# Four of the eight block sums per set of a 7-product SwiGLU layer moved from VectorE to accumulating SBUF transfers, the products reordered, and two more weight buffers

## The chip, the cores and the metric

The kernel runs on one core of a Trainium2 chip. The metric is the device time of one execution in microseconds (us). TensorE (PE) multiplies, with its weight loads as a sequence of their own (PEld); VectorE (DVE) and ScalarE (ACT) work element by element; GpSimd (POOL) and SyncE (SP) issue transfers (DMA). Each engine takes its instructions in order, and semaphores hold it back until what it needs is there.

## The reference, cut to what matters

A trunk of 4 layers over 256 tokens of width 1024. Each layer has an FFN, a token mixer with memory attention, and a second FFN, each wrapped in RMS norms:

```python
def swiglu_ffn(x, w_gate_up, w_down):
    gate, up = jnp.split(x @ w_gate_up, 2, axis=-1)
    return (jax.nn.silu(gate) * up) @ w_down
...
for i in range(DEPTH):
    x = x + 0.5 * rms_norm(swiglu_ffn(rms_norm(x, g[0]), ffn_w_gate_up[i, 0], ffn_w_down[i, 0]), g[1])
    h = rms_norm(x, g[2])
    ...
    x = x + rms_norm(y, g[3])
    x = x + 0.5 * rms_norm(swiglu_ffn(rms_norm(x, g[4]), ffn_w_gate_up[i, 1], ffn_w_down[i, 1]), g[5])
```

The hidden width of the FFN is 2816, everything is fp32, and there are 8 FFNs. The change is in the FFNs alone, but for the place in which some small tiles of other parts lie.

## The kernel before, in words

**Units of weight.** The weights are read once, in units of 512 KB (128 partitions x 1024 fp32). SP's queue loads a unit (L240) into one of `RAW` = 3 buffers named `raw`. ACT rounds it to a high part `hi` (L309) and DVE takes the rest as a low part `lo` (L310), both in rings of `RING` = 10 buffers. A product is then three matmuls, hi*hi, lo*hi and hi*lo (L334 to L336). `pump` (called from `slot`, after every unit that PE has taken) issues splits as far ahead as the ring has free places. A split of a `raw` frees that buffer and issues the next load of a `raw`.

**An FFN.** The 2816 hidden columns are done in 6 sets, 0 to 5, of 512 columns (the last of 256). For an ordinary set PE makes the gate half `g` (4 units) and the up half `u` (4 units) in PSUM banks named `rot`, of which there are 4; ACT and DVE make silu(gate) * up from them in tiles `T` (L537, L538, L727). PE transposes T (`turned`, L557) two units later, and the hidden columns go through the down matrix into two double banks `acc` (L684, `fill(n)`: n units of the down matrix, 24 matmuls for two). These fills are put between other products, so that PE has work while something is waited for.

**The seven-product sets.** Sets 2 and 4 of each FFN (`SEVEN`), 16 sets in all, do gate and up together as a 2x2 block product with 7 instead of 8 block products (`seven`, L626 to L661). The four weight blocks b11, b12, b21, b22 lie in four tiles `quad` of two halves of 512 KB each, 8 loads per set, which `slot` issues in the order b11, b21, b12, b22 (`load_quad`). The left operands are input blocks or sums of these (`sums`, made once per FFN, L599). The right operands are blocks or sums of them, made in place by `operand` with a DVE addition of 128x1024 (L277) for each half: b11+=b12, b11+=b22, b12+=b22, b21+=b11, so 8 additions per set. Each product, numbered op 0 to 6, is split like any unit and takes 12 matmuls of 512 columns, 6 for each half (L615). PE's order in a set is: op 0 into bank a; op 1 into bank b; the transposes of the set before (two banks); op 2 into bank c; op 3 into bank a; fill(2); op 4 into a; fill(2); op 5 into a; op 6 into c. DVE and ACT take from them: a snapshot P1 of a (ACT, L623), P1+b (DVE, L635, which reads bank b for the last time), a snapshot U2, a snapshot U3, c-U3 (DVE, L646), the silu of a and a product (L653), c-U2 (L658) and the product that gives the first half of T (L659).

Each engine's instructions are put in order by a scheduler when the program is built; within that, the order comes from the Python code and from the plan of units (`ffn_chunks`), by which the splits are issued. A bank, ring place or buffer is reused as soon as its last reader is done.

**Around it.** A boundary between stages makes norms and transposes (L373 to L385, L399). `gain` loads the norm gains. `setup2` loads and prepares the memory for the mixers. `mem_chunk` loads pieces of the memory into `memraw`.

Of the kernel before, what the change touches and what calls it, by code (L numbers as in the profile page):

```python
# [10 lines left out]
F32 = mybir.dt.float32  # L11
# [22 lines left out]
RAW = 3  # L34
# [27 lines left out]
def ffn_chunks(l, f):  # L62
# [8 lines left out]
    for s in range(SETS):  # L71
        if s in SEVEN:
            for ops, n in (((0, 1, 2, 3), 2), ((4,), 2), ((5, 6), 0)):
                order += [("S", l, f, s, op, h) for op in ops for h in range(2)]
                fill(n)
            continue
# [127 lines left out]
class Trunk:  # L204
# [53 lines left out]
    def load_quad(self):  # L258
# [16 lines left out]
    def operand(self, op, h):  # L275
        b11, b12, b21, b22 = (t if t is None else t[:, h, :] for t in self.quad)
        add = lambda x, y: self.nc.vector.tensor_tensor(out=x, in0=x, in1=y, op=ALU.add)  # L277
# [73 lines left out]
    def gain(self, l, n, tag):  # L351
        t = self.main.tile([P, D], F32, tag=tag, name=tag)
# [3 lines left out]
    def ln_stages(self, st, t, ps, post_scale, post_eps, gpost, gpre):  # L356
# [3 lines left out]
        junk = lambda: self.main.tile([P, D], BF16, tag="junk", name="junk")  # L360
# [11 lines left out]
        def s1():  # L372
            nc.scalar.activation(out=junk(), in_=ps, func=AF.Square, scale=post_scale, accum_out=ss)  # L373
# [6 lines left out]
        def s3():  # L380
            nc.scalar.activation(out=junk(), in_=x, func=AF.Square, scale=1 / 32, accum_out=ss2)
# [47 lines left out]
    def setup(self):  # L429
# [4 lines left out]
        self.gpre = self.gain(0, 0, "gpre")  # L434
# [18 lines left out]
    def setup2(self):  # L453
# [3 lines left out]

        def loads():
# [3 lines left out]
        def squares(t):  # L462
            m = self.main.tile([P, D], F32, tag="gpost", name="memrow")
            nc.sync.dma_start(out=m, in_=io["mem"][t * P:(t + 1) * P, :])
            ss = self.small.tile([P, 1], F32, tag="ss", name="ss", bufs=8)
            nc.scalar.activation(out=self.main.tile([P, D], BF16, tag="junk", name="junk"), in_=m, func=AF.Square,
# [3 lines left out]
        def inverse():  # L470
            ps = self.rot()
            for t in range(2):
                d = self.main.tile([P, SEQ], F32, tag="memraw", name="memf", bufs=2)
# [55 lines left out]
    def ffn(self, l, f, post_next, pre_next, last=False):  # L529
        nc, tc = self.nc, self.tc  # L530
        with tc.tile_pool(name=f"ffn{l}{f}", bufs=1, reuse_waits="tile") as fp:
# [61 lines left out]
            def sums():  # L593
# [3 lines left out]
                for dst, a, b, op in ((x22, x21, x22, ALU.subtract), (x21, x11, x21, ALU.subtract),  # L597
                                      (x11, x22, x11, ALU.subtract), (x12, x12, x11, ALU.add)):
                    tt(out=dst, in0=a, in1=b, op=op)  # L599
                    y = tuple(fp.tile([P, 4, P], F32R, tag=n, name=n, bufs=4) for n in ("sh", "sl"))  # L600
# [6 lines left out]
                return a11, a12, S1, S2, S3, a22, S4  # L607
# [721 lines left out]
```

## Time and profile before

| what | us |
|---|---|
| median of 3 runs | 1900.68 (1900.43 to 1908.29) |
| profiled execution | 1902.04 |
| its span, first to last instruction | 1900.2 |
| PE busy | 1858.8 (98%) |
| DVE busy | 1514.9 (80%) |
| ACT busy | 1085.9 (57%) |
| POOL busy | 59.8 (3%) |
| mean granted TensorE clock | 0.999 |

The span of the profiled execution is 1.84 us shorter than its time, which has what lies around the span too. A row of instruction groups in the profile gives line, engine, operation, out <- in, shape and count, then busy time, mean of one in ns, and the idle time of that engine just before them with what ended it. The lines of SP issue transfers ("SPq"); "us to landing" is from the issue to the data being there. In a timeline the columns are start, duration and the instruction; several like ones in a row are one line (x8), and idle time just before is in brackets. Consecutive matmuls overlap, so their start times and not their durations show the pace.

### The profile page before, as it was taken

The numbers are of one execution on the slowest core, as the hardware profiler recorded it, in microseconds if no ns is written. First come the engines' busy times: TensorE is split into PE (matmuls) and PEld (weight loads), VectorE is DVE, ScalarE is ACT, GpSimd is POOL, SyncE is SP. The second block draws the span as 40 slices with busy tenths as digits, with TensorE's granted clock in tenths as the row PEclk, the third lists the DMA queues.
The fourth block names the chain that finished last, engine by engine and source line by source line (L and its number), as shares of the span: only waits on it lengthen the run. The fifth ranks groups of instructions, "written<-read, shape, count | busy, mean of one in ns | idle before, by whom it ended". The sixth has DMA issues, their size and how long they took to land.

```text
span 1900.2 us, 25015 instructions
## 1 busy us (share of the span) xinstructions
PE 1858.8 (98%) x9406; PEld 1550.4 (82%) x9406; DVE 1514.9 (80%) x1828; ACT 1085.9 (57%) x1469; POOL 59.8 (3%) x115
## 2 busy tenths in 40 slices
PE   7999999999999999999999999999999999999998
PEld 5888888787878897888888889888888878988886
DVE  6987888896879768889697966878877886878894
ACT  5655656564656545655565656555556555656562
POOL 0000100000000000000000000000000000100000
PEclk9999999999999999999999999999999999999999
DMA  8646747545663663754566357275476535747632
GB/s 295 235 167 200 233 156 266 205 140 176 233 222 115 199 203 111 266 198 145 180 231 233 112 185 238 102 246 184 151 229 227 189 127 183 243 156 244 220 105 86
DMA packets 103865, 362.65 MB, mean 191 GB/s; under 512 B 12084, under 2 KB 16576, under 8 KB 103616
## 3 DMA queue, kind: packets, MB, share of 16 engines
q1 hardware_dynamic: 103568, 359.47, 56.5%
q8 instruction: 74, 1.21, 0.3%
q0 software_dynamic: 176, 1.59, 0.2%
q14 instruction: 47, 0.39, 0.1%
HBM read 359.95 MB, written 1.06 MB: 190 GB/s over the span
## 4 chain that ended last, share of the span: by engine, by line
PE 60%; DVE 17%; DMA 12%; ACT 5%; issue 4%; POOL 1%; ACTq 0%; SPq 0%; DVEq 0%
PE acc L684 15%; DMA raw<-in_w 12%; PE rot L615 9%; PE rot L334 9%; PE rot L336 9%; PE rot L335 9%; DVE lo L310 9%; ACT hi L309 4%; DVE quad L277 3%; PE acc L944 3%; PE rot L557 1%; PE rot L399 1%; PE rot L848 1%; DVE x L378 1%; PE rot L880 1%
## 5 line engine op out<-in xcount | busy, mean ns | idle before, releaser
L310 DVE TENSOR_TENSOR lo<-raw,hi 128x1024 fp32r<-128x1024 f32 (+1 forms) x515 | 624.4, 1219 | 216.9 <-ACT hi L309 207.5
L309 ACT ACTIVATE hi<-raw 128x1024 fp32r<-128x1024 f32 (+1 forms) x515 | 542.1, 1055 | 397.0 <-DMA raw<-in_w 259.0
L334 PE MATMUL rot<-hi,xth 128*128 128x512 f32 (+3 forms) x1072 | 414.9, 387 | 2.5 <-ACT hi L309 1.6
L336 PE MATMUL rot<-hi,xtl 128*128 128x512 f32 (+3 forms) x1072 | 411.6, 384 | 1.2 <-DVE xtl L310 1.1
L335 PE MATMUL rot<-lo,xth 128*128 128x512 f32 (+3 forms) x1072 | 411.6, 384 | 0.0
L309 ACT ACTIVATE hi<-quad 128x1024 fp32r<-128x1024 f32 x224 | 232.7, 1056 | 156.5 <-DVE quad L277 83.4
L310 DVE TENSOR_TENSOR lo<-quad,hi 128x1024 fp32r<-128x1024 f32 x224 | 269.4, 1220 | 7.2 <-ACT hi L309 6.2
L334 PEld LDWEIGHTS rot<-hi,xth 128*128 128x128 f32 x1072 | 202.1, 189 | 41.4 <-ACT hi L309 2.1
L336 PEld LDWEIGHTS rot<-hi,xtl 128*128 128x128 f32 x1072 | 201.9, 188 | 41.3 <-DVE xtl L310 2.3
L335 PEld LDWEIGHTS rot<-lo,xth 128*128 128x128 f32 x1072 | 202.1, 189 | 38.2
L684 PE MATMUL acc<-lo,hh 128*128 128x512 f32 x640 | 198.9, 390 | 0.0
L684 PE MATMUL acc<-hi,hh 128*128 128x512 f32 x640 | 198.0, 390 | 0.0
L684 PE MATMUL acc<-hi,hl 128*128 128x512 f32 x640 | 197.2, 389 | 0.0
L277 DVE TENSOR_TENSOR quad<-quad 128x1024 f32<-128x1024 f32 x128 | 154.2, 1220 | 0.9
L684 PEld LDWEIGHTS acc<-hi,hl 128*128 128x128 f32 x640 | 120.1, 188 | 25.0 <-DVE hl L310 0.2
L684 PEld LDWEIGHTS acc<-lo,hh 128*128 128x128 f32 x640 | 120.2, 188 | 24.8
L684 PEld LDWEIGHTS acc<-hi,hh 128*128 128x128 f32 x640 | 119.5, 188 | 24.3
L615 PE MATMUL rot<-hi,sh 128*128 128x512 f32 x256 | 103.0, 402 | 6.8 <-DVE snap L635 6.8
L615 PE MATMUL rot<-lo,sh 128*128 128x512 f32 x256 | 100.0, 391 | 0.0
L615 PE MATMUL rot<-hi,sl 128*128 128x512 f32 x256 | 97.4, 390 | 0.0
L374 DVE TENSOR_TENSOR rows<-acc,gpost 128x1024 f32<-128x1024 f32 x24 | 29.3, 1222 | 74.9 <-ACT junk L373 74.8
L615 PE MATMUL rot<-hi,xtl 128*128 128x512 f32 x192 | 74.8, 389 | 0.0
(212 smaller groups left out, 2439.8 us busy)
## 6 DMA issues: line engine op xcount, KB each, us to landing
raw<-in_w SPq DMA_DIRECT2D x504, 512.0 KB, 4.3
quad<-in_w SPq DMA_DIRECT2D x128, 512.0 KB, 5.8
gpre<-in_norm_g SPq DMA_DIRECT2D x12, 512.0 KB, 5.1
gpost<-in_norm_g SPq DMA_DIRECT2D x12, 512.0 KB, 5.4
memraw<-in_mem_t SPq DMA_DIRECT2D x32, 128.0 KB, 3.2
raw<-in_w SPq DMA_DIRECT2D x8, 384.0 KB, 3.5
sw<-in_sw SPq DMA_DIRECT2D x2, 768.0 KB, 8.1
cb<-cd POOLq DMA_DIRECT2D x1, 1536.0 KB, 9.9
```

Of the source, the lines that this page charges most:

```text
L277: add = lambda x, y: self.nc.vector.tensor_tensor(out=x, in0=x, in1=y, op=ALU.add)
L309: self.nc.scalar.activation(out=hi, in_=src, func=AF.Copy)
L310: self.nc.vector.tensor_tensor(out=lo, in0=src, in1=hi.bitcast(F32), op=ALU.subtract)
L334: mm(out, a[0], b[0], start=start, stop=False)
L335: mm(out, a[0], b[1], start=False, stop=False)
L336: mm(out, a[1], b[0], start=False, stop=stop)
L374: nc.vector.tensor_tensor(out=rows(), in0=ps, in1=gpost, op=ALU.mult)
L378: nc.vector.scalar_tensor_tensor(out=x, in0=rows(), scalar=r, in1=x, op0=ALU.mult, op1=ALU.add)
L399: nc.tensor.transpose(ps[:, (k - k0) * P:(k - k0 + 1) * P], rows[:, k * P:(k + 1) * P], self.ident)
L615: nc.tensor.matmul(ps, a[i], w[j][:, kk, :], start=fresh and h == kk == i == j == 0, stop=h == kk == i == 1, skip_group_check=True)
L684: mm(ys[t][:, n * 512:(n + 1) * 512], x, y[:, 0, n * 512:(n + 1) * 512], start=(j == 0 and x is a[0] and y is w[0]), stop=(j == NF - 1 and ...
L944: self.nc.tensor.matmul(o["y"][t][:, h * 512:(h + 1) * 512], x, y[:, 0, h * 512:(h + 1) * 512], start=(j == 0 and x is a[0] and y is w[0]) ...
```

## The change

**What it does.** Of the four sums of weight blocks per set, two are made by transfers: `gather` issues from GpSimd's queue a transfer from one SBUF tile into another with accumulation. b12+=b22 is issued for each half right after the load of b22's half; b21+=b11 after DVE's addition for op 2. That is 4 transfers of 512 KB per set, 64 in all. DVE keeps b11+=b12 (op 2; b12 has b22 in it by then) and gets b11-=b22 (op 4, a subtraction), together 4 instructions per set, so 64 in place of 128. Since op 2 needs b22 now, splits from op 2 on are held until all 8 loads of the set have been issued (`quads_for`).

The order of products changes: op 2, 3 and 4 are now S2 times (b11+b12+b22), S3 times (b12+b22) and S1 times (b11+b12). Op 2 goes into bank a, followed by fill(2); op 3 goes into bank a; a new bank c is taken only then, for op 4; op 5 goes into a, op 6 into c; and fill(2) closes the set.

Tiles are put elsewhere: `junk` and `memraw` share the four `snap` buffers, the gains lie in the buffers of the left sums (tag `S`, which replaces `sh` and `sl`) or in tiles of the mixer, and `memrow` lies in `rows`. The loads of the gains and `setup2` are issued after the second seven-product set of an FFN. `RAW` is 5 instead of 3.

```diff
-RAW = 3
+RAW = 5
...
-            for ops, n in (((0, 1, 2, 3), 2), ((4,), 2), ((5, 6), 0)):
+            for ops, n in (((0, 1, 2), 2), ((3, 4, 5, 6), 2)):
...
         self.fetch(self.quad[q][:, h, :], key)
+        if q == 3:
+            self.gather(self.quad[1][:, h, :], self.quad[3][:, h, :])
+
+    def gather(self, x, y):
+        self.nc.gpsimd.dma_start(out=x, in_=y, accum_op=ALU.add)
...
-        return max(0, len(self.quad_loads) - (QUADS - (2 * min(key[4], 3) + key[5] + 1)))
+        return max(0, len(self.quad_loads) - (QUADS - ((2 * key[4] if key[4] < 2 else 6) + key[5] + 1)))
...
-        add = lambda x, y: self.nc.vector.tensor_tensor(out=x, in0=x, in1=y, op=ALU.add)
         if op == 2:
-            add(b11, b12)
-        elif op == 3:
-            add(b11, b22)
+            self.nc.vector.tensor_tensor(out=b11, in0=b11, in1=b12, op=ALU.add)
+            self.gather(b21, b11)
         elif op == 4:
-            add(b12, b22)
-        elif op == 5:
-            add(b21, b11)
-        return (b11, b21, b11, b11, b12, b21, b22)[op]
+            self.nc.vector.tensor_tensor(out=b11, in0=b11, in1=b22, op=ALU.subtract)
+        return (b11, b21, b11, b12, b11, b21, b22)[op]
...
-    def gain(self, l, n, tag):
-        t = self.main.tile([P, D], F32, tag=tag, name=tag)
+    def dump(self):
+        return self.main.tile([P, D], BF16, tag="snap", name="junk", bufs=4)
+
+    def gain(self, l, n, t):
...
-                return a11, a12, S1, S2, S3, a22, S4
+                return a11, a12, S2, S3, S1, a22, S4
...
-                a, b, c = self.rot(), self.rot(), self.rot()
+                a, b = self.rot(), self.rot()
...
                 turned(s - 1)
-                product(s, 2, c, True)
-                product(s, 3, a, False, keep("U2"))
+                product(s, 2, a, False, keep("U2"))
                 fill(2)
+                product(s, 3, a, False, keep("U3"))
+                c = self.rot()
 
                 def c22():
-                    v["U3"] = snap(a)
                     tt(out=v["U3"], in0=c, in1=v["U3"], op=ALU.subtract)
 
-                product(s, 4, a, False, c22)
-                fill(2)
+                product(s, 4, c, True, c22)
...
                 product(s, 6, c, False, c12)
+                fill(2)
...
-            if (l, f) != (0, 0):
-                self.bg.append(gains)
...
+                    if s == max(SEVEN):
+                        self.bg.append(gains)
+                    if s == max(SEVEN) and (l, f) == (0, 0):
+                        self.bg.extend(self.setup2())
```

**How it moves the instructions.** The places are in set 2 of the second FFN of layer 2, here called set 10, since ten seven-product sets come before it. A number after a name is that of the buffer's tile, and what stands in brackets is what the instruction waits for: a semaphore of an engine (Activation is ACT), of a loading queue (DMAHW) or of a GpSimd transfer (DMASW).

On PE before, from the transposes of the set before on; rot_11760 is bank a, rot_11761 is b, rot_11762 is c, and the two between are those of the transposes:

```order
L557 MATMUL rot_11816<-ident_74,T_11510 128x128 [waits DVE_49]
L557 MATMUL rot_11816<-ident_74,T_11510 128x128 x3
L557 MATMUL rot_11823<-ident_74,T_11511 128x128 [waits DVE_49]
L557 MATMUL rot_11823<-ident_74,T_11511 128x128 x3
L615 MATMUL rot_11760<-hi_11716,sh_11499 128x512 [waits Activation_49]
L615 MATMUL rot_11760<-lo_11717,sh_11499 128x512
L615 MATMUL rot_11760<-hi_11716,sl_11500 128x512
L615 MATMUL rot_11760<-hi_11716,sh_11499 128x512
L615 MATMUL rot_11760<-lo_11717,sh_11499 128x512
L615 MATMUL rot_11762<-hi_11682,sh_11489 128x512 [waits DVE_49]
L615 MATMUL rot_11762<-lo_11683,sh_11489 128x512
L615 MATMUL rot_11762<-hi_11682,sl_11490 128x512
```

The first matmul of op 2, into bank c, waits for DVE, which has to free a bank; the scheduler has put 5 of op 3's matmuls into bank a ahead of it. On PE in the changed kernel at the same place, where rot_11739 is bank a:

```order
L563 MATMUL rot_11790<-ident_74,T_11489 128x128 [waits DVE_49]
L563 MATMUL rot_11790<-ident_74,T_11489 128x128 x3
L563 MATMUL rot_11797<-ident_74,T_11490 128x128 [waits DVE_49]
L563 MATMUL rot_11797<-ident_74,T_11490 128x128 x3
L622 MATMUL rot_11739<-hi_11659,sums_11480 128x512 [waits Activation_49]
L622 MATMUL rot_11739<-lo_11660,sums_11480 128x512
L622 MATMUL rot_11739<-hi_11659,sums_11480 128x512 x2
L622 MATMUL rot_11739<-lo_11660,sums_11480 128x512
```

Op 2 follows the transposes in bank a, and waits for ACT alone (its `hi`, and the snapshot P1). On PE in the changed kernel, the end of op 5 and the first matmul of op 6, where rot_11886 is bank c, which op 4 has filled:

```order
L622 MATMUL rot_11739<-hi_11810,xtl_11162 128x512
L622 MATMUL rot_11739<-hi_11810,xth_11161 128x512
L622 MATMUL rot_11739<-lo_11811,xth_11161 128x512
L622 MATMUL rot_11739<-hi_11810,xtl_11162 128x512
L622 MATMUL rot_11886<-hi_11822,sums_11484 128x512 [waits DVE_49]
```

Op 6 adds to bank c and waits for DVE, which reads that bank in L653 (c-U3, L646 before). The 12 matmuls of op 5 lie between op 4 and op 6; before, they were op 5's and those of a fill.

On DVE before, from the second split of op 0 to the last sums of the second half; quad_11526 is b11, quad_11585 b21, quad_11626 b12, quad_11663 b22:

```order
L310 TENSOR_TENSOR lo_11629<-quad_11526,hi_11628 128x1024 [waits PE_49,Activation_49]
L277 TENSOR_TENSOR quad_11526<-quad_11526,quad_11626 128x1024 [waits DMAHW6_49,DVE_49]
L310 TENSOR_TENSOR lo_11646<-quad_11585,hi_11645 128x1024 [waits Activation_49]
L277 TENSOR_TENSOR quad_11526<-quad_11526,quad_11626 128x1024 [waits DMAHW2_49,DVE_49]
L310 TENSOR_TENSOR lo_11666<-quad_11585,hi_11665 128x1024 [waits Activation_49]
L277 TENSOR_TENSOR quad_11626<-quad_11626,quad_11663 128x1024 [waits DVE_49]
L310 TENSOR_TENSOR lo_11683<-quad_11526,hi_11682 128x1024 [waits Activation_49]
L277 TENSOR_TENSOR quad_11626<-quad_11626,quad_11663 128x1024 [waits DVE_49]
L277 TENSOR_TENSOR quad_11526<-quad_11526,quad_11663 128x1024 [waits DVE_49]
L310 TENSOR_TENSOR lo_11700<-quad_11526,hi_11699 128x1024 [waits Activation_49]
L277 TENSOR_TENSOR quad_11585<-quad_11585,quad_11526 128x1024 [waits DVE_49]
L310 TENSOR_TENSOR lo_11717<-quad_11526,hi_11716 128x1024 [waits Activation_49]
```

All eight sums of a set stand here and in the rows behind, each with a wait for a load or for DVE's own result. On DVE in the changed kernel, where quad_11505 is b11, quad_11560 b21, quad_11601 b12, quad_11638 b22:

```order
L283 TENSOR_TENSOR quad_11505<-quad_11505,quad_11601 128x1024 [waits DMASW2_49,DVE_49]
L544 SCALAR_TENSOR_TENSOR T_11490<-T_11490,rot_11492 128x512 [waits Activation_49]
L311 TENSOR_TENSOR lo_11604<-quad_11505,hi_11603 128x1024 [waits DMAHW7_49,PE_49,Activation_49]
L311 TENSOR_TENSOR lo_11621<-quad_11560,hi_11620 128x1024 [waits Activation_49]
L283 TENSOR_TENSOR quad_11505<-quad_11505,quad_11601 128x1024 [waits DMASW3_49,DVE_49]
L311 TENSOR_TENSOR lo_11642<-quad_11560,hi_11641 128x1024 [waits Activation_49]
L311 TENSOR_TENSOR lo_11660<-quad_11505,hi_11659 128x1024 [waits Activation_49]
L286 TENSOR_TENSOR quad_11505<-quad_11505,quad_11638 128x1024 [waits DMAHW1_49,DMASW4_49,DVE_49]
L311 TENSOR_TENSOR lo_11678<-quad_11505,hi_11677 128x1024 [waits Activation_49]
L286 TENSOR_TENSOR quad_11505<-quad_11505,quad_11638 128x1024 [waits DMAHW4_49,DMASW5_49,DVE_49]
L311 TENSOR_TENSOR lo_11696<-raw_11456,hi_11695 128x1024 [waits DMAHW7_49,Activation_49]
L735 TENSOR_TENSOR T_11489<-T_11489,rot_11624 128x512 [waits PE_49]
```

Additions (L283) and subtractions (L286) now wait for GpSimd's transfers: the additions for b12+=b22, the subtractions for b21+=b11, which reads b11 before the subtraction may write it. Behind the last of them stand a split and the L735 that makes the T which PE's transposes (L563) read.

On SP the last load of the set, b22's second half, stands in this place right behind the load of the `raw` whose buffer comes free with the last split of a `raw` that DVE makes ahead of the set's first block (lo_11563, two rows of `hl` ahead of the first split of b11). It stands so in sets 0, 1, 2, 10 and 14; in the others it stands about ten loads earlier.

More of the change, by code (lines that the diff above doesn't have):

```diff
@@ L359, in ln_stages @@
             st["rows"] = None
-        junk = lambda: self.main.tile([P, D], BF16, tag="junk", name="junk")
         ss = self.small.tile([P, 1], F32, tag="ss", name="ss", bufs=8)
@@ L372, in s1 @@
         def s1():
-            nc.scalar.activation(out=junk(), in_=ps, func=AF.Square, scale=post_scale, accum_out=ss)
+            nc.scalar.activation(out=self.dump(), in_=ps, func=AF.Square, scale=post_scale, accum_out=ss)
             nc.vector.tensor_tensor(out=rows(), in0=ps, in1=gpost, op=ALU.mult)
@@ L380, in s3 @@
         def s3():
-            nc.scalar.activation(out=junk(), in_=x, func=AF.Square, scale=1 / 32, accum_out=ss2)
+            nc.scalar.activation(out=self.dump(), in_=x, func=AF.Square, scale=1 / 32, accum_out=ss2)
             self.rsqrt(r2, ss2, self.eps1)
@@ L433, in setup @@
         nc.sync.dma_start(out=self.x[0], in_=io["x"][:P, :])
-        self.gpre = self.gain(0, 0, "gpre")
+        self.gpre = self.gain(0, 0, self.main.tile([P, 2, D], F32, tag="mgh", name="gpre")[:, 0, :])
         nc.sync.dma_start(out=self.ident, in_=io["ident"])
@@ L456, in setup2 @@
         self.R = c.tile([P, SEQ], F32, name="R")
+        both = []
         def loads():
@@ L462, in squares @@
         def squares(t):
-            m = self.main.tile([P, D], F32, tag="gpost", name="memrow")
+            if t == 0:
+                both.append(self.main.tile([P, 2, D], F32, tag="rows", name="memrow"))
+            m = both[0][:, t, :]
             nc.sync.dma_start(out=m, in_=io["mem"][t * P:(t + 1) * P, :])
             ss = self.small.tile([P, 1], F32, tag="ss", name="ss", bufs=8)
-            nc.scalar.activation(out=self.main.tile([P, D], BF16, tag="junk", name="junk"), in_=m, func=AF.Square,
+            nc.scalar.activation(out=self.dump(), in_=m, func=AF.Square,
                                  scale=1 / 32, accum_out=ss)
@@ L472, in inverse @@
             for t in range(2):
-                d = self.main.tile([P, SEQ], F32, tag="memraw", name="memf", bufs=2)
+                d = self.main.tile([P, SEQ], F32, tag="snap", name="memf", bufs=4)
                 nc.vector.tensor_scalar(out=d[:, :P], in0=self.ident, scalar1=self.r_mem[:, t:t + 1], scalar2=None,
@@ L599, in sums @@
                     tt(out=dst, in0=a, in1=b, op=op)
-                    y = tuple(fp.tile([P, 4, P], F32R, tag=n, name=n, bufs=4) for n in ("sh", "sl"))
+                    y = fp.tile([P, 2, 4, P], F32R, tag="S", name="sums", bufs=4)
+                    y = (y[:, 0], y[:, 1])
                     self.split(*(v.rearrange("p a b -> p (a b)") for v in y), dst)
@@ L667, in gains @@
             def gains():
-                gn["post"] = self.gain(l, post_next[0], "gpost")
+                tile = lambda n: fp.tile([P, D], F32, tag="S", name=n, bufs=4)
+                gn["post"] = self.gain(l, post_next[0], tile("gpost"))
                 if pre_next:
-                    gn["pre"] = self.gain(*pre_next, "gpre")
-            if (l, f) != (0, 0):
-                self.bg.append(gains)
+                    gn["pre"] = self.gain(*pre_next, tile("gpre"))
             ys = [self.acc() for _ in range(2)]
@@ L706, in ffn @@
                     seven(s)
-                    if s == min(SEVEN) and (l, f) == (0, 0):
-                        self.bg.extend(self.setup2() + [gains])
+                    if s == max(SEVEN):
+                        self.bg.append(gains)
+                    if s == max(SEVEN) and (l, f) == (0, 0):
+                        self.bg.extend(self.setup2())
                     if s == min(SEVEN) and (l, f) == (0, 1):
@@ L747, in mem_chunk @@
     def mem_chunk(self, k):
-        m = self.main.tile([P, SEQ], F32, tag="memraw", name="memraw", bufs=2)
+        m = self.main.tile([P, SEQ], F32, tag="snap", name="memraw", bufs=4)
         self.nc.sync.dma_start(out=m, in_=self.io["mem_t"][k * P:(k + 1) * P, :])
@@ L962, in gains @@
     def gains(self, l):
-        return self.gain(l, 3, "gpost"), self.gain(l, 4, "gpre")
+        return tuple(self.gain(l, n, self.mp.tile([P, D], F32, name=f"g{n}")) for n in (3, 4))
     def mix_a(self, mp, l, j, xt):
```

## The prediction, on record before the changed kernel was run

> **What bounds the kernel now.** I read the page first (busy shares, the chain that ended last), then PE's waits, then the timeline of PE and DVE around one seven-product set, then stretches and transfer times. The busy rows and the chain:
>
> ```profile
> PE 1858.8 (98%) x9406; PEld 1550.4 (82%) x9406; DVE 1514.9 (80%) x1828; ACT 1085.9 (57%) x1469; POOL 59.8 (3%) x115
> ...
> PE 60%; DVE 17%; DMA 12%; ACT 5%; issue 4%; POOL 1%; ACTq 0%; SPq 0%; DVEq 0%
> ```
>
> PE is busy for 1858.8 of 1900.2 us. The change leaves the number of matmuls as it is, so at most the other 41.4 us can go. PE's waits, as total, times and longest:
>
> ```profile
> PE rot L399 <- DVE rows L385: 15.5, 11, 8.4
> PE rot L615 <- DVE snap L635: 6.8, 7, 1.8
> PE rot L557 <- DVE T L659: 4.8, 6, 1.5
> PE rot L557 <- DVE T L719: 2.1, 5, 0.7
> PE rot L334 <- ACT hi L309: 1.6, 1, 1.6
> ```
>
> L399 and L719 belong to boundaries and the last set, whose work the change doesn't touch. The rows it can touch are the second, third and fifth: 6.8 + 4.8 + 1.6 = 13.2 us.
>
> **The bank wait (L635).** Set 10 on PE, start and duration first:
>
> ```profile
> 1316.31 0.39 PE L615 MATMUL rot<-hi,xtl 128*128 128x512 f32 x1
> 1316.55 1.03 PE L557 MATMUL rot<-ident,T 128*128 128x128 f32 x8
> 1317.34 0.48 PE L615 MATMUL rot<-hi,sh 128*128 128x512 f32 x1
> ...
> 1318.34 0.39 PE L615 MATMUL rot<-lo,sh 128*128 128x512 f32 x1
> 1320.12 0.50 PE L615 MATMUL rot<-hi,sh 128*128 128x512 f32 x1 [1.39 <-DVE snap L635]
> ```
>
> and on DVE at the same time:
>
> ```profile
> 1318.25 1.22 DVE L310 TENSOR_TENSOR lo<-raw,hi 128x1024 fp32r<-128x1024 f32 x1
> 1319.38 0.68 DVE L635 TENSOR_TENSOR snap<-snap,rot 128x512 f32<-128x512 f32 x1
> ```
>
> Op 1 is done at about 1316.55, but DVE takes its queued splits first and frees bank b only at 1319.38 + 0.68 = 1320.06. PE starts at 1320.12: it waited for the bank, not for weights. In the new order op 2 goes into bank a, and a third bank is first wanted for op 4. Between lie op 2, fill(2) and op 3. Their price:
>
> ```profile
> 1332.72 0.61 PE L684 MATMUL acc<-hi,hh 128*128 128x512 f32 x2
> ...
> 1338.16 0.39 PE L615 MATMUL rot<-hi,xth 128*128 128x512 f32 x1
> ...
> 1340.88 0.39 PE L615 MATMUL rot<-hi,sh 128*128 128x512 f32 x1
> ```
>
> The fill takes 1338.16 - 1332.72 = 5.44 us, one product (op 5, up to the first matmul of op 6) 1340.88 - 1338.16 = 2.72. So L635 gets 2.72 + 5.44 + 2.72 = 10.9 us more, against a lag of 3.5 (1320.06 - 1316.55). **Term: -6.8.**
>
> **The wait at the set's end (L659).** PE's next transposes, and DVE before them:
>
> ```profile
> 1349.67 1.09 PE L557 MATMUL rot<-ident,T 128*128 128x128 f32 x8 [0.47 <-DVE T L659]
> ```
> ```profile
> 1347.20 0.68 DVE L658 TENSOR_TENSOR snap<-rot,snap 128x512 f32<-128x512 f32 x1
> 1347.80 1.22 DVE L310 TENSOR_TENSOR lo<-raw,hi 128x1024 fp32r<-128x1024 f32 x1
> 1348.93 0.69 DVE L659 TENSOR_TENSOR T<-T,snap 128x512 f32<-128x512 f32 x1
> ```
>
> Now a fill of 5.44 us lies between op 6 and these transposes, and the longest such wait was 1.5. **Term: -4.8.** The fill isn't additional: it stood after op 4. What loses its cover there comes below.
>
> **The startup.** PE's one wait for ACT's split, at the end of the first half:
>
> ```profile
> 20.89 0.60 ACT L537 ACTIVATE T<-rot 128x512 f32<-128x512 f32 x1 [5.25 <-PE rot L336]
> 21.38 2.00 ACT L309 ACTIVATE hi<-raw 128x1024 fp32r<-128x1024 f32 x2
> 22.48 0.50 PE L334 MATMUL rot<-hi,xth 128*128 128x512 f32 x1 [1.63 <-ACT hi L309]
> ```
>
> ACT was free for 5.25 us, and yet the next split stood behind L537, which needs PE's finished bank. With 5 raw buffers the first five units can be split ahead of it. **Term: -1.6**; bounds 0 and -1.6.
>
> **What is removed from DVE.** 64 of its 128 additions go, of this group, and the splits beside it don't:
>
> ```profile
> L277 DVE TENSOR_TENSOR quad<-quad 128x1024 f32<-128x1024 f32 x128 | 154.2, 1220 | 0.9
> ```
>
> That is 64 x 1.22 = 78 us of DVE, 4.9 a set. On PE's path it is worth nothing by itself: no row of PE's waits names a split of `quad`. It buys lead. RAW = 5 likewise, beyond the startup. The moved loads of gains and of `setup2` have the whole last set and the rest of the down matrix for cover, several landings of 5 us long; if that cover failed they would be a wait of some us at a boundary, and I cost them at nothing.
>
> **What is added on PE's path.** Op 6 adds to the bank that c-U3 reads. Its cover falls from op 5 and a fill, 8.16 us, to op 5 alone, 2.72. L646 in set 10:
>
> ```profile
> 1333.85 0.68 DVE L646 TENSOR_TENSOR snap<-rot,snap 128x512 f32<-128x512 f32 x1
> ```
>
> Op 4 ended at about 1332.72, so bank c was free 1333.85 + 0.68 - 1332.72 = 1.81 us later: 0.9 to spare. But the splits queued ahead of it on DVE may hold it as long as L635, 3.5 us. Bounds: 0, and (3.5 - 2.72) x 16 sets = 12.5 us. It is nearest to L646's own row, since it is the same instruction behind the same kind of splits; I take 2.0, a wait in some of the sets. The snapshot U3 has the same cover of 2.72 (op 4) and is one ACT instruction, so it goes with this term.
>
> **The transfers.** No accumulating transfer is in the trace. The nearest rows, KB each and us from issue to landing:
>
> ```profile
> raw<-in_w SPq DMA_DIRECT2D x504, 512.0 KB, 4.3
> quad<-in_w SPq DMA_DIRECT2D x128, 512.0 KB, 5.8
> ...
> cb<-cd POOLq DMA_DIRECT2D x1, 1536.0 KB, 9.9
> ...
> out_x<-x SPq DMA_DIRECT2D x2, 512.0 KB, 2.6
> ```
>
> Call the time from GpSimd's issue to landing G. Lower bound 2.6 (512 KB out of SBUF on quiet queues); upper bound 2 x 5.8 = 11.6, since an accumulation reads its target too. I take 5.8, the row of like size in the same phase of the set. How loaded that phase is (PE, PEld, DVE, ACT, POOL, clock, DMA share, GB/s):
>
> ```profile
> 1285.00:1312.00 27.00, 27.00 (x120) 22.34 (x119) 24.96 (x25) 12.79 (x16) 0.00 (x0) 1.00 0.31 108
> 1312.00:1344.00 32.00, 30.61 (x139) 25.14 (x138) 23.90 (x24) 21.16 (x25) 0.00 (x0) 1.00 0.79 282
> ```
>
> The sums are due in the first stretch, where the DMA engines are used to 0.31: there is room. The Trainium skill ("DMA: Bandwidth & Descriptors", "Anatomy of one DMA") gives about 2.0 us plus bytes over 436 GB/s for a transfer from GpSimd's queue, by estimate 3.2 us here; it says nothing of the accumulation, no run here shows it, and by it the sum would be the same.
>
> How late may G be? In set 10 the last half of b22 is issued after the last raw split ahead of the set, and on DVE that split comes before this row:
>
> ```profile
> 1287.56 1.28 DVE L310 TENSOR_TENSOR hl<-rot,hh 128x512 fp32r<-128x512 f32 x2
> 1308.94 1.28 DVE L727 TENSOR_TENSOR T<-T,rot 128x512 f32<-128x512 f32 x2
> ```
>
> By 1287.6 plus two issues (0.8) plus 5.8 it has landed, 1294.2; then the gather b12+=b22 (G), DVE's addition and the split of b21 (2 x 1.22), the gather b21+=b11 (G), the subtraction that waits for it, a split (2 x 1.22), and L727 (L735 now, 1.28). DVE goes in order, so T is ready at 1294.2 + 2G + 6.2 = 1300.4 + 2G. PE's transposes need it at 1316.55. So G may be (1316.55 - 1300.4) / 2 = 8.1 us in the five sets where the last load stands so late, and more in the others, where only the second gather can hold DVE. At 5.8 it costs nothing: DVE waits, but out of lead. **Term: 0.**
>
> **Sum.** 1902.04 - 6.8 - 4.8 - 1.6 + 2.0 = 1890.84 for the profiled execution. That one was 1.36 above the median (1902.04 - 1900.68), so 1889.5, or 0.59% faster. What a measurement of this kernel can tell from no change is about 0.5%, 9.5 us: below 1891.2 is faster, above 1910.2 slower. Its own range is 1886 (no new waits) to 1895 (no startup term, some 4 us more of new waits).
>
> **Rivals.**
>
> *Waits replaced.* The splits ahead of L646's successor hold bank c, and op 6 waits in most sets, up to the 12.5 us above: 1889.5 - 2.0 + 12.5 = 1900.0 at most, about 1897 at three quarters. For it: the L635 lag of 3.5 behind one queued split. Against it: L646's own 1.81, and DVE has 4.9 us a set less to do.
>
> *Late gathers, slower than before.* DVE stands in order behind an addition or subtraction whose transfer is late; behind it stands the L735 that the transposes need. From G = 8.1 on each of the five sets loses 2 (G - 8.1). At G = 11.6 that is 5 x 7.0 = 35 us: 1889.5 + 35 = 1924.5. It is slower by over 0.5% from G = 10.2 on (10 x 2.1 = 21 us). For it: a transfer that adds may cost two, 64 of them move another 33.5 MB, and the L277 row shows that DVE never waited here before (0.9 us in all). Against it: the 0.31. The Trainium skill ("SBUF — State Buffer", "SBUF: two separate sides") says that GpSimd cannot write descriptors while DVE runs an instruction in a two-port mode, which would add to G; the splits are of no kind that it names for this, and no row of before shows it. With one split of 1.22 us added, G would be 7.0 and the sum the same.
>
> *No effect of RAW and the lead.* If the waits at L635 and L659 only moved to the boundaries (L399), the time would be near 1900. The boundaries wait for PE's own last products, so I give that little; it is counted with the first rival.
>
> **Chances.** Forecast 0.63 (0.45 below 1891.2, 0.18 above); waits replaced 0.18, all within 0.5%; late gathers 0.19 (0.18 slower, 0.01 not). Faster 0.45, same 0.37, slower 0.18. The range 1884 to 1911 leaves out the late gathers above (0.17) and 0.03 below, for a lead that also shortens the startup.
>
> **What would show it.** Right: no PE wait on P1+b (L642 now) or on the T of a set's end (L665); a small one for op 6 on c-U3 (L653); DVE's sums at 64 instructions with some us of idle time before them put down to the transfers; gathers landing within 8 us of their issue. Wrong: gathers above 10 us, PE transposes waiting for L735 in sets 0, 1, 2, 10 and 14, or op 6 waiting in most sets.

## The result, and the profile after

The changed kernel took 1881.24 us (median of 4 runs, 1880.50 to 1882.07) where the kernel before took 1902.38 on the same chip: a ratio of 0.9884, 95% interval 0.986 to 0.9908. On a second chip the ratio was 0.9909 (0.9896 to 0.9921). The profiled execution took 1880.50 us, 21.5 less than the 1902.04 of before; 11.2 less had been forecast, and the time lies below the range of 1884 to 1911. One of the six executions of a later experiment, the kernel with every transfer issued twice, took 2316.4 us at a granted clock of 0.752, and its ratio is formed without it.

The busy rows and the chain of the changed kernel:

```profile
PE 1851.9 (99%) x9406; PEld 1550.9 (83%) x9406; DVE 1440.9 (77%) x1764; ACT 1089.3 (58%) x1469; POOL 121.7 (6%) x179
...
PE 88%; DVE 4%; DMA 3%; issue 2%; ACT 2%; POOL 1%; SPq 0%; ACTq 0%; DVEq 0%; POOLq 0%
```

The span is 1878.3, so PE idles for 26.4 us instead of 41.4. Its busy time is 6.9 us less too (1851.9 instead of 1858.8), with the same 9406 matmuls. The chain now runs through PE for 88% of the span, through DVE for 4 (17 before) and through transfers for 3 (12 before). PE's waits, as total, times and longest:

```profile
PE rot L401 <- DVE rows L387: 15.4, 11, 8.3
PE acc L690 <- DVE hl L311: 0.9, 1, 0.9
PE rot L856 <- DVE p L910: 0.7, 1, 0.7
PE rot L336 <- DVE lo L311: 0.6, 2, 0.3
PE rot L335 <- ACT hi L310: 0.4, 1, 0.4
PE rot L563 <- DVE T L586: 0.4, 1, 0.4
```

L401 is the boundary wait, as large as before (15.5). The rows for P1+b (6.8), for the T of a set's end (4.8) and for the T of the last set (L719, 2.1) are gone, and no row has op 6 waiting for c-U3. Set 10 on PE, then DVE's P1+b (L642 now):

```profile
1302.73 0.39 PE L622 MATMUL rot<-hi,xtl 128*128 128x512 f32 x1
1302.96 1.03 PE L563 MATMUL rot<-ident,T 128*128 128x128 f32 x8
1303.75 0.48 PE L622 MATMUL rot<-hi,sums 128*128 128x512 f32 x1
...
1306.57 0.62 PE L690 MATMUL acc<-hi,hh 128*128 128x512 f32 x2
```
```profile
1304.29 0.68 DVE L642 TENSOR_TENSOR snap<-snap,rot 128x512 f32<-128x512 f32 x1
```

Op 2 runs through from 1303.75 to the fill at 1306.57. L642 ends at 1304.97, 2.0 us after op 1 (1302.96), where it was 3.5 before.

The transfers, KB each and us to landing, and the DVE groups that wait for them (busy, mean ns, idle before):

```profile
quad<-quad POOLq DMA_DIRECT2D x64, 512.0 KB, 6.0
```
```profile
L286 DVE TENSOR_TENSOR quad<-quad 128x1024 f32<-128x1024 f32 x32 | 39.1, 1225 | 22.3 <-DMA quad<-quad 14.3 <-issue 5.1 <-DVE lo L311 2.7
L283 DVE TENSOR_TENSOR quad<-quad 128x1024 f32<-128x1024 f32 x32 | 39.1, 1221 | 23.1 <-DMA quad<-quad 22.7
```

A transfer with accumulation lands 6.0 us after its issue (5.8 had been taken), and DVE stands idle for some 45 us in front of the sums, 37.0 of them put down to the transfers. No row of PE's waits names these sums.

### The profile page after: what moved, and what is told of

It is laid out like the page before. It is cut to its first block, busy times and chain, and to the rows that moved or that the text cites. A ratio compares the mean times of both kernels' runs of the same rounds, so it can differ in the third digit from the quotient of the medians.

```text
span 1878.3 us, 25267 instructions
## 1 busy us (share of the span) xinstructions
PE 1851.9 (99%) x9406; PEld 1550.9 (83%) x9406; DVE 1440.9 (77%) x1764; ACT 1089.3 (58%) x1469; POOL 121.7 (6%) x179
## 4 chain that ended last, share of the span: by engine, by line
PE 88%; DVE 4%; DMA 3%; issue 2%; ACT 2%; POOL 1%; SPq 0%; ACTq 0%; DVEq 0%; POOLq 0%
PE acc L690 23%; PE rot L622 16%; PE rot L335 13%; PE rot L336 13%; PE rot L337 13%; PE acc L952 3%; DMA raw<-in_w 2%; PE rot L563 2%; DVE lo L311 1%; PE rot L401 1%; PE rot L856 1%; ACT hi L310 1%; PE acc L874 1%; PE rot L888 1%; DVE rows L387 1%
## 5 line engine op out<-in xcount | busy, mean ns | idle before, releaser
L310 ACT ACTIVATE hi<-raw 128x1024 fp32r<-128x1024 f32 (+1 forms) x515 | 537.2, 1053 | 328.6 <-DMA raw<-in_w 110.7
L622 PE MATMUL rot<-hi,sums 128*128 128x512 f32 x512 | 166.9, 392 | 0.0
L622 PEld LDWEIGHTS rot<-hi,sums 128*128 128x128 f32 x512 | 96.2, 188 | 19.5
L269 POOL DMA_DIRECT2D quad<-quad x64 | 55.9, 889 | 724.3 <-DVE lo L311 345.3
L622 PE MATMUL rot<-lo,sums 128*128 128x512 f32 x256 | 99.7, 389 | 0.0
L349 POOL TENSOR_TENSOR r<-ss,thin 128x1 f32<-128x1 f32 x48 | 23.4, 488 | 904.6 <-ACT junk L375 812.7
```

The source lines that it names most:

```text
L269: self.nc.gpsimd.dma_start(out=x, in_=y, accum_op=ALU.add)
L310: self.nc.scalar.activation(out=hi, in_=src, func=AF.Copy)
L349: g.tensor_tensor(out=out, in0=ss, in1=eps_tile, op=ALU.add)
L622: nc.tensor.matmul(ps, a[i], w[j][:, kk, :], start=fresh and h == kk == i == j == 0, stop=h == kk == i == 1, skip_group_check=True)
```

## The experiments

"Buffers" are those named `raw`. The kernels of one paragraph that are compared in us ran on one chip; otherwise ratios to the kernel before on the same chip are compared. The changed kernel has 0.9884 and 0.9909 on two chips, and the one with all sums on DVE 0.9904 and 0.9887, so a difference of less than some 0.3% between ratios from different chips shows nothing. The theories, as they stand in the expectations: A, the new order of PE brings the gain; B, the lead of DVE and of the loads does; C, the five buffers alone do; D, the transfers are needed; E, the transfers cost.

| kernel | order | sums | buffers | median us | ratio to before (95%) |
|---|---|---|---|---|---|
| changed (second chip) | new | 2 of 4 by transfer | 5 | 1881.32 | 0.9909 (0.9896 to 0.9921) |
| e3b_dve_sums | new | DVE | 5 | 1877.21 | 0.9887 (0.9873 to 0.9902) |
| e7_raw5_only | old | DVE | 5 | 1879.33 | 0.9897 (0.9884 to 0.9909) |
| e2_old_order | old | 2 of 4 by transfer | 5 | 1880.43 | 0.9921 (0.9908 to 0.9933) |
| e11_raw4 | old | DVE | 4 | 1891.28 | 0.9969 (0.9952 to 0.9986) |
| e10_moves_only | old | DVE | 3 | 1918.46 | 1.0109 (1.0083 to 1.0134) |
| e9_old_gather_raw3 | old | 2 of 4 by transfer | 3 | 1910.56 | 1.0075 (1.0049 to 1.0101) |
| e5_order_only | new | DVE | 3 | 1905.51 | 1.0039 (1.0024 to 1.0054) |
| e1_raw3 | new | 2 of 4 by transfer | 3 | 1941.33 | 1.0244 (1.0217 to 1.027) |

All of these have the tiles moved as in the changed kernel. The sums aren't in the same place in all: before, `operand` issues one with each of op 2 to op 5; the old-order kernels of this table issue the last three together with op 3, and the new-order ones without transfers issue three with op 2.

### Three buffers in the changed kernel

```diff
-RAW = 5
+RAW = 3
```

> Changed kernel with 3 raw buffers instead of 5, all else kept. Theory A (the order of PE brings the gain at the banks and the set ends; the two buffers bring only the startup, 3.9 us, and the wait of the last set's transposes, 2.1 us): 1885 to 1888, PE's waits for P1+b and for the T of a set's end stay gone. Theory B (the lead of DVE and of the loads brings the gain): 1892 or more, and waits at the set ends come back.

Measured: 1941.33 us, 1.0244. Everything else of the change, without the two buffers, is 2.4% slower than before. Its waits on PE:

```profile
PE acc L690 <- ACT hh L310: 13.6, 11, 3.2
PE acc L874 <- ACT qm L840: 7.8, 2, 4.4
PE rot L622 <- DVE snap L653: 7.5, 5, 2.4
PE acc L690 <- DVE hl L311: 6.7, 12, 2.2
PE rot L563 <- DVE T L727: 4.7, 6, 1.2
```

Here op 6 does wait for c-U3 (L653, 7.5), the fills wait for the transposed T, and the L727 row is the T of the last set (L719 before). Theory A falls on the time, but one part of it holds: no row for P1+b (L642) or for the T of a set's end (L665) has come back. B said the right direction but not the size.

### The old order with transfers and five buffers

```diff
-            for ops, n in (((0, 1, 2), 2), ((3, 4, 5, 6), 2)):
+            for ops, n in (((0, 1, 2, 3), 2), ((4,), 2), ((5, 6), 0)):
...
+        elif op == 3:
+            self.nc.vector.tensor_tensor(out=b11, in0=b11, in1=b22, op=ALU.add)
+            self.gather(b12, b22)
+            self.gather(b21, b11)
...
+                product(s, 2, c, True)
+                product(s, 3, a, False, keep("U2"))
+                fill(2)
```

> Changed kernel with the old order of products, banks and fills; two of the four sums still by transfers, issued with op 3; 5 raw buffers. Theory A: the bank wait and the set-end wait are back, about 1895 to 1898 (only startup and the last set stay better). Theory B: 1883 to 1887.

Measured: 1880.43, 0.9921. The gain doesn't need the new order: the old one has it too.

### All sums on DVE

```diff
-        if q == 3:
-            self.gather(self.quad[1][:, h, :], self.quad[3][:, h, :])
...
         if op == 2:
-            self.nc.vector.tensor_tensor(out=b11, in0=b11, in1=b12, op=ALU.add)
-            self.gather(b21, b11)
+            add(b12, b22)
+            add(b11, b12)
+            add(b21, b11)
```

> Changed kernel with the two transferred sums made by DVE additions again, in the same place in the order (ahead of op 2); 5 raw buffers, new order. Theory A: 1880 to 1884, the transfers were only a way to save DVE work that PE does not wait for. Theory B: 1888 to 1895, DVE is 78 us busier and late at the set ends.

Measured: 1877.27, 0.9904 (0.989 to 0.9918). To compare it with the changed kernel without a difference of chips, both ran again side by side:

> The changed kernel once more, beside the next three on one chip, so that they can be compared without the difference of chips. Both theories: about 0.988 of before.

> Changed kernel with all sums on DVE again, a second time, beside the changed kernel. Theory C (five raw buffers bring the gain; with them neither the transfers nor the order matter): within 0.3% of the changed kernel on this chip. Theory D (the transfers are needed for the gain): slower than it by 0.5% or more. Theory E (the transfers cost): faster by about 3 us, the difference of the two profiled spans (1878.3 and 1875.1).

Measured: 1881.32 (1879.70 to 1884.23) with the transfers, 1877.21 (1876.49 to 1878.48) without; the runs don't overlap. Theory D falls and E holds: the transfers cost 4.1 us here. This kernel is faster than both the one before and the changed one, though DVE is busy for 1513.3 us in its first profile. Where the 4.1 us lie isn't shown. DVE's waits for the transfers are one candidate; another is the loads of weights beside them, since ACT's splits wait 118.8 us for loads of `raw` with the transfers and 60.9 without, on this chip.

### The buffers alone

```diff
-            self.gather(b12, b22)
-            self.gather(b21, b11)
+            self.nc.vector.tensor_tensor(out=b12, in0=b12, in1=b22, op=ALU.add)
+            self.nc.vector.tensor_tensor(out=b21, in0=b21, in1=b11, op=ALU.add)
```

The diff is against the old-order kernel above.

> Old order of products, banks and fills, all eight sums on DVE, tiles moved as in the changed kernel, and 5 raw buffers: of the change only the buffers and the room for them. Theory C: within 0.3% of the changed kernel, 0.988 to 0.992 of before. Theory A, of order and raw buffers together: 0.995 or more.

Measured: 1879.33, 0.9897. Its waits on PE:

```profile
PE rot L400 <- DVE rows L386: 15.2, 11, 8.2
PE rot L621 <- DVE snap L641: 0.5, 1, 0.5
PE rot L335 <- DVE lo L310: 0.3, 1, 0.3
PE rot L334 <- ACT hi L309: 0.3, 1, 0.3
```

In the old order, with all eight sums on DVE, the bank wait is down from 6.8 to 0.5 and the wait at the set's end is gone. Five buffers are enough to remove what the prediction gave to the order. Theory C holds. The new order is worth 2.1 us beyond that (1879.33 against 1877.21 on the same chip, runs apart).

### The same with three and with four buffers

```diff
-RAW = 5
+RAW = 3
```

> Old order, all sums on DVE, 3 raw buffers: of the change only the tiles that lie elsewhere and the later loads of gains and memory. Theory C (raw buffers): 0.997 to 1.003 of before, with its waits (P1+b, T of the set's end, the slow start) still there. If the moved tiles and loads bring part of the gain, 0.995 or less.

> As with raw buffers alone (old order, all sums on DVE), but 4 of them. Theory C: between 0.990 and 1.000 of before; ACT's wait for raw loads between the 259.0 us of 3 buffers and what 5 leave (under 40).

Measured: 1.0109 and 0.9969, with 0.9897 for five. Each buffer counts, and the kernel with the moved tiles and three is 1.1% slower than before, which neither theory had said. What ACT waits for points to the mechanism. ACT's splits waiting for a load of `raw` (total, times, longest), before, then moved with three buffers, with four, with five:

```profile
ACT hi L309 <- DMA raw<-in_w: 259.0, 226, 3.7
```
```profile
ACT hi L309 <- DMA raw<-in_w: 261.3, 217, 4.4
```
```profile
ACT hi L309 <- DMA raw<-in_w: 86.5, 94, 2.6
```
```profile
ACT hi L309 <- DMA raw<-in_w: 27.6, 33, 2.7
```

A `raw` is loaded again only after its split, and a load takes 4.3 us to land. With three buffers ACT finds its next unit not landed 217 to 226 times. ACT and DVE go in order, so what is queued behind such a split is late as well; the next experiment shows it in set 10. The row tells where to look and not what it is worth: the first two rows are alike, and the second kernel is 1.1% slower.

### Five buffers in the kernel before

```diff
-RING = 10
-RAW = 3
+RING = 9
+RAW = 5
```

The diff is against the kernel before; one place of the ring pays for the two buffers.

> The kernel before with 5 raw buffers, paid for by one place of the split ring (9 instead of 10), nothing else changed. Theory C (raw buffers): 0.989 to 0.994 of before, and PE's waits for P1+b, for the T of a set's end and for that of the last set gone. If the gain needs the room for 5 buffers and the ring's lead as well: 0.998 or more.

Measured: 1884.56, 0.9931 (0.9916 to 0.9946). PE's waits:

```profile
PE rot L399 <- DVE rows L385: 15.1, 11, 8.0
PE rot L334 <- ACT hi L309: 1.2, 2, 1.0
PE rot L336 <- DVE xtl L310: 1.1, 1, 1.1
PE rot L334 <- ACT xth L309: 1.1, 1, 1.1
PE rot L336 <- DVE lo L310: 0.8, 1, 0.8
```

L635, L659 and L719 are gone in the kernel before as well, by the buffers alone and with less lead in the ring. ACT's wait for loads is 25.6 us, and the chain that ended last, 60% PE, 17% DVE and 12% transfers before, is now:

```profile
PE 94%; DVE 2%; issue 1%; POOL 1%; ACT 1%; DMA 0%; SPq 0%; ACTq 0%; DVEq 0%
```

At the end of set 10 the late loads can be seen directly. Before, ACT's splits wait for loads of `raw` (2.47 us here, and 1.45, 0.35 and 1.20 for three of the next), DVE's wait for ACT's, and L659 stands behind them in DVE's order:

```profile
1335.99 1.06 ACT L309 ACTIVATE hi<-raw 128x1024 fp32r<-128x1024 f32 x1 [2.47 <-DMA raw<-in_w]
```
```profile
1337.08 1.22 DVE L310 TENSOR_TENSOR lo<-raw,hi 128x1024 fp32r<-128x1024 f32 x1 [2.55 <-ACT hi L309]
```

With five buffers no split of that stretch waits for a load of `raw`, and T is ready at 1334.93, 2.2 us before PE's transposes want it:

```profile
1334.25 0.68 DVE L659 TENSOR_TENSOR T<-T,snap 128x512 f32<-128x512 f32 x1
1337.16 1.03 PE L557 MATMUL rot<-ident,T 128*128 128x128 f32 x8
```

The bank wait (L635) in the same set is less direct. DVE has no pause in the timeline there before, from 1291.84 to the end of L635 at 1320.06: it works off a queue. The first sum of the set, before and with five buffers:

```profile
1296.45 1.22 DVE L277 TENSOR_TENSOR quad<-quad 128x1024 f32<-128x1024 f32 x1
```
```profile
1281.98 1.23 DVE L277 TENSOR_TENSOR quad<-quad 128x1024 f32<-128x1024 f32 x1
```

That is 20.1 us ahead of the end of op 1 (1316.55) before, and 24.2 ahead of it (1306.15) with five buffers. But the scheduler's order differs too: the split of a `raw` that DVE makes right ahead of L635 before (1318.25 in the prediction) stands behind it with five buffers. How much of the bank wait is lead and how much is this order wasn't tried.

### The order alone

```diff
-RAW = 5
+RAW = 3
```

The diff is against the kernel with all sums on DVE.

> New order of products, banks and fills, all sums on DVE, 3 raw buffers. Theory A: 0.992 of before (the bank wait and the set-end wait go, 11.6 us of 1900, and a part of it is given back). Theory C: 1.00 or slower than before, since the loads are late as they were with 3 buffers and transfers (1.024).

Measured: 1.0039 (1.0024 to 1.0054), where the old order had 1.0109. With late loads the new order is worth 0.7% (theory A's 0.8%), from a worse start; with early ones 0.1%. PE's waits show what the prediction expected of the order: P1+b (5.9 us with the old order and three buffers) and the T of a set's end (5.0) have no row, and op 6 on c-U3 has one of 2.8.

### The fill put back

```diff
-            for ops, n in (((0, 1, 2), 2), ((3, 4, 5, 6), 2)):
+            for ops, n in (((0, 1, 2), 2), ((3, 4), 2), ((5, 6), 0)):
...
                 product(s, 4, c, True, c22)
+                fill(2)
...
                 product(s, 6, c, False, c12)
-                fill(2)
```

> Changed kernel with the second fill put back between op 4 and op 5. Theory A: the wait of the transposes for the T of a set's end comes back, 1881 + 6 = 1887. Theory B: no difference, 1881 to 1883, since DVE is early enough by its lead.

Measured: 1888.75, 0.9964 (0.9951 to 0.9977). In this kernel the wait for the T of a set's end is back, 7.9 us in 5 waits. So the closing fill covers something in the new order with transfers, as theory A said of it, while the old order with five buffers doesn't need it. Why the two differ wasn't tried.

### Transfers with three buffers, old order

```diff
-RAW = 5
+RAW = 3
```

The diff is against the old-order kernel with transfers.

> Old order with two sums by transfers (issued with op 3) and 3 raw buffers. If the transfers hurt with 3 buffers because the new order needs b22 and its transfer before op 2: 0.995 to 1.005 of before. If transfers beside late loads hurt in any order (as 1.024 with the new order): 1.01 or more.

Measured: 1.0075 (1.0049 to 1.0101), against 1.0109 without transfers: they don't hurt there. In the new order, with three buffers, they raise 1.0039 to 1.0244. One difference between the two is when the transfers are wanted: b12+=b22 before op 2's split in the one, before op 4's in the other. That this makes the time wasn't tried alone.

### Every transfer twice

```diff
         self.nc.gpsimd.dma_start(out=x, in_=y, accum_op=ALU.add)
+        self.nc.gpsimd.dma_start(out=x, in_=y, accum_op=ALU.add)
```

> Changed kernel (5 raw buffers, new order) with every accumulating transfer issued twice, one after the other, so that its result holds the addend twice: a sum of the weight blocks is then another one. The time to the second landing is about 11 to 12 us. By the prediction's chain (break-even 8.1, five sets, two transfers) about 1881 + 5 x 2 x 3.5 = 1916. If five raw buffers move the chain's start ahead and give DVE more lead: 1884 to 1895.

Measured: 1955.9 us, 1.0309 (1.028 to 1.0338). One transfer still lands in 6.1 us, so by estimate a pair in about 12. DVE in the first set of the run, then PE:

```profile
81.65 1.23 DVE L287 TENSOR_TENSOR quad<-quad 128x1024 f32<-128x1024 f32 x1 [3.25 <-DMA quad<-quad]
86.92 1.23 DVE L287 TENSOR_TENSOR quad<-quad 128x1024 f32<-128x1024 f32 x1 [4.04 <-DMA quad<-quad]
88.06 0.68 DVE L643 TENSOR_TENSOR snap<-snap,rot 128x512 f32<-128x512 f32 x1
```
```profile
88.89 0.76 PE L623 MATMUL rot<-hi,sums 128*128 128x512 f32 x1 [7.15 <-DVE snap L643]
```

The rival "late gathers" is real: subtractions that wait for a transfer hold P1+b behind them in DVE's order, and PE stands for 7.15 us. Its price was put too low (1916): it counted T alone in five sets. PE's fills wait too, 19.1 us for ACT's `hh` and 15.7 for DVE's `hl`, and PE is busy for 1879.3 us, 27.4 more than in the changed kernel, with as many matmuls. Doubling the transfers costs some 75 us against the changed kernel (chips differ by some us). It doubles what they move as well as their time to land, and ACT's splits wait 172.5 us for loads of `raw` instead of 110.7, so the price isn't that of the landing time alone.

### Which move costs with three buffers

```diff
-            if (l, f) != (0, 0):
-                self.bg.append(gains)
...
-                    if s == min(SEVEN) and (l, f) == (0, 0):
-                        self.bg.extend(self.setup2() + [gains])
+                    if s == max(SEVEN) and (l, f) == (0, 0):
+                        self.bg.extend(self.setup2())
+                    if s == max(SEVEN):
+                        self.bg.append(gains)
```

> The kernel before with the loads of gains and the preparation of the memory issued after the second seven-product set, nothing else changed. If these later loads make the moved kernel with 3 buffers slow: 1.005 to 1.011 of before. If not: 0.998 to 1.002.

```diff
-        junk = lambda: self.main.tile([P, D], BF16, tag="junk", name="junk")
+        junk = lambda: self.main.tile([P, D], BF16, tag="snap", name="junk", bufs=4)
...
-        m = self.main.tile([P, SEQ], F32, tag="memraw", name="memraw", bufs=2)
+        m = self.main.tile([P, SEQ], F32, tag="snap", name="memraw", bufs=4)
```

> The kernel before with the small tiles junk and memraw in the four snapshot buffers, nothing else changed. If this sharing makes the moved kernel with 3 buffers slow: 1.005 to 1.011 of before. If not: 0.998 to 1.002.

Measured: 1.0019 (1.0005 to 1.0034) and 1.0017 (1.0001 to 1.0034): neither makes the 1.1%. In the kernel with the moves alone, SP waits for PE before a load of gains, since these lie in the buffers of the left sums, which PE reads to the end of the second set; loads of `raw` stand behind it on SP. The row there, and in the changed kernel:

```profile
SPq L355 <- PE rot L621: 32.3, 15, 3.6
```
```profile
SPq L356 <- PE rot L622: 65.6, 8, 11.7
```

The gains in tiles of their own, and the same without that edit beside it:

```diff
-                tile = lambda n: fp.tile([P, D], F32, tag="S", name=n, bufs=4)
+                tile = lambda n: self.main.tile([P, D], F32, tag=n, name=n)
```

> Moved tiles, old order, all sums on DVE, 3 raw buffers, but the FFN's gains in tiles of their own in place of the buffers of the left sums. If SP's wait for those buffers, with raw loads behind it, makes that kernel slow: 0.998 to 1.004 of before. If not: 1.008 to 1.013, as without this edit.

> The same kernel without that edit, a second time, beside it: 1.008 to 1.013 of before.

Measured: 1908.32, 1.0064 (1.0047 to 1.0081), and 1916.09, 1.0112 (1.0083 to 1.014). That is 8 of the 19 us between the moved kernel and before. SP's wait for those buffers has no row any more. It was neither of the two outcomes expected; what the other 11 us are stays open. Not tried were the gains of the mixers and `memrow` in their new places, and the sums, of which the last two come earlier in these kernels than before.

## Why the prediction was right and wrong

**The step that failed** is the one on what is removed from DVE: "On PE's path it is worth nothing by itself: no row of PE's waits names a split of `quad`", and behind it "RAW = 5 likewise, beyond the startup". For DVE's work this was right: taking it away brought nothing. For the buffers it was wrong. Two more were priced at 1.6 us. They are worth 0.69% in the layout of before (1897.05 to 1884.56, 12.5 us), and with the moved tiles 2.1% (1.0109 to 0.9897). The error was to stop at the name in PE's wait row. L635 and L659 were the last links. L659 stood in order behind splits of `raw`, and these behind late loads; L635 stood at the end of a queue that DVE began later than with five buffers. The page of before pointed there twice: ACT's splits idle for 259.0 us in front of loads of `raw`, and the chain that ended last, quoted at the head of the prediction, runs through DVE for 17% and through transfers for 12%, which the prediction didn't follow up.

**The bank wait, -6.8, and the set's end, -4.8.** Both went, in full. The order alone removes them, as the prediction argued (new order, three buffers: no row for either); with the moved tiles that brought 1.0109 to 1.0039. Five buffers alone remove them too (0.5 and 0 left in the old order). The two causes overlap, and the prediction named only the one that adds 2.1 us when the other is there.

**The last set's T (L719, 2.1).** The prediction called it untouched. It went, with five buffers in the layout of before as well.

**The startup, -1.6.** The same number of matmuls stands ahead of op 0 of the first set. Its first matmul before, with five buffers in the layout of before, and changed:

```profile
73.54 0.39 PE L615 MATMUL rot<-hi,xth 128*128 128x512 f32 x1
```
```profile
72.01 0.39 PE L615 MATMUL rot<-hi,xth 128*128 128x512 f32 x1
```
```profile
69.73 0.39 PE L622 MATMUL rot<-hi,xth 128*128 128x512 f32 x1
```

The wait of 1.63 us that the term named is gone with five buffers in the layout of before. Every trace with three buffers has a wait for a split at that place (1.55 to 1.92), so the term was right. The other 2 us are two pauses of PE, 0.83 and 1.12 us at 11.18 and 13.52, which the prediction didn't name. They stand in the kernels in which `junk` has one buffer of its own, and in none in which it shares the four `snap` buffers, the experiment with this sharing alone included. The start times themselves are rough: two traces of one kernel, with moved tiles and three buffers, have 71.05 and 72.87.

**Op 6 on c-U3, +2.0.** It cost nothing; no row has PE waiting for L653 with five buffers. With three the wait exists, 2.8 us with all sums on DVE and 7.5 with transfers, so 2.0 was the right order of size for a kernel whose loads are late.

**The transfers, 0.** G came out at 6.0 for 5.8, below the break-even, so the slower rival did not come in. That the row of plain loads fitted so well was in part luck, since the same transfer took 4.4 in the old order. And the transfers cost 4.1 us where the prediction had 0.

**The sum.** Forecast -11.2, measured -21.5 in the profiled executions, 21.9 in the spans. PE's idle time gives 15.0 of that: the sum of its wait rows falls by 15.4, of which L635 and L659 are 11.6, L719 2.1 and three at the start 3.5, against 1.8 of small ones that come. The other 6.9 is PE's busy time. The prediction took it as fixed by the number of matmuls ("at most the other 41.4 us can go"), and it wasn't: a matmul after a wait is slow itself, 0.33 us to the next start (1320.12 to 1320.45) where 0.23 is usual, and so are PE's first ones; these aren't added up here. By ratios, the five buffers in the layout of before are worth 0.69%, the new order 0.1% beyond them, and the transfers cost 0.2%. What the moved tiles and the tenth place of the ring add to five buffers, 0.9897 against 0.9931 on another chip, is about as large as the difference of chips and stays open. A small slip besides: without new waits the prediction's sum gives 1887.5, not the 1886 that it states.

## What to carry to other kernels

Where engines go in order, the name in a wait row is the last link: look at what the named engine was doing before it, and at the largest "idle before" on that engine and on the one that feeds it, here ACT's 259.0 us in front of loads. The rows of the bottleneck engine tell how much can be gained (L635, L659, L719 and the wait for ACT's split, 15.3 us here) and not by which remedy. The row of late loads points to a remedy and not to its worth: bringing 259.0 us down to 25.6 was worth 12.5. So try the buffer count alone, first. A step that is taken off a busy engine and put on a transfer need not be worth anything: here it cost 4.1 us, and some 75 when each transfer was doubled.

## What the runs showed of the hardware

**TensorE's first microseconds are slow, for a time that varies.** Starts of matmuls of 512 columns in the changed kernel, and in a second execution of the same kernel:

```profile
11.57 0.63 PE L335 MATMUL rot<-hi,xth 128*128 128x512 f32 x1
12.00 0.56 PE L336 MATMUL rot<-lo,xth 128*128 128x512 f32 x1
12.39 0.39 PE L337 MATMUL rot<-hi,xtl 128*128 128x512 f32 x1
12.63 0.40 PE L335 MATMUL rot<-hi,xth 128*128 128x512 f32 x1
```
```profile
13.54 0.63 PE L336 MATMUL rot<-lo,xth 128*128 128x512 f32 x1
13.97 0.47 PE L337 MATMUL rot<-hi,xtl 128*128 128x512 f32 x1
14.28 0.40 PE L335 MATMUL rot<-hi,xth 128*128 128x512 f32 x1
```

The pace is 0.43 us for a matmul at best until 12.39 in the one and until 14.28 in the other, 4.1 and 6.1 us after PE's first instruction (8.32 and 8.22), with no pause between; then it is 0.23. In the other traces without a pause at the start it takes from 3.7 us (every transfer twice) to 8.2 (all sums on DVE, second time). The clock column reads 1.00 in these stretches. The Trainium skill ("TensorE: Matmul & The Clock Gate", "Part 1: The HAM clock gate") says that the array starts at half its clock and comes to the full one after some 3.4 us of sustained work; the trace agrees with the half pace, but the time was 3.7 to 8.2 us here.

**A long pause costs more than its own length.** With every transfer doubled, after the pause of 7.15 us (stretch, PE, PEld, DVE, ACT, POOL, clock, DMA share, GB/s):

```profile
80.00:90.00 10.00, 2.57 (x10) 1.48 (x8) 4.31 (x5) 2.82 (x4) 0.00 (x0) 0.82 0.73 226
90.00:100.00 10.00, 9.76 (x29) 7.29 (x30) 9.62 (x10) 6.57 (x8) 0.00 (x0) 0.67 0.64 237
```

The clock falls to 0.67 in the 10 us behind it, and PE does 29 matmuls there, where 46 stand in the stretches from 60 to 70 and from 100 to 110. The 17 that are missing are some 4 us, by an estimate at 0.23 us each. It is one pause in one kernel. The mean clock of that kernel is 0.985, where the changed one has 0.998, and this is part of why late transfers cost more than the 1916 that had been expected.

**An accumulating transfer** of 512 KB from SBUF to SBUF landed in 6.0 us in the new order, and in 4.4 in the old one. The Trainium skill's formula for a transfer from GpSimd's queue ("DMA: Bandwidth & Descriptors", "Anatomy of one DMA") gave an estimate of 3.2; it has no term for accumulation, and the trace decides.
